# Max-pool and subtract in fp32: a loop by tile, with tiles of five rows in five slots and a first tile in pieces of 1, 1 and 2 rows

## The chip, the cores and the metric

One core of a Trainium2 chip runs the kernel; the other cores are idle. A transfer below is one DMA issue of the kernel. The 16 DMA engines of the core share each transfer, and a packet is what one engine moves at a time: the run of one partition, or the 4-byte completion at the end (in the profile before, 68 transfers make 9792 packets, 9 on each engine per transfer). The metric is the time of one execution on the device in microseconds (us). All times compared here are of undisturbed ("fast") runs unless a sentence says otherwise. The span of a profile, from the first to the last instruction of the program, is some 1.8 us shorter than the time of the same run.

## The reference

```python
x: float32, shape (8, 64, 256, 256)          # B, C, H, W
x_r = x.reshape(B, C, H // 8, 8, W // 8, 8)
pooled = x_r.max(axis=(3, 5))                # maximum of each 8 x 8 window
return x - (pooled repeated 8 times along H and W)
```

Each element is read once (134.2 MB) and written once (134.2 MB). The arithmetic is two passes over data that is on chip.

## The kernel before

Eight image lines form one row of 2048 numbers (8 KB), which holds whole windows. There are 16384 such rows. A tile of *n* rows puts *n* consecutive rows into each of the 128 partitions, so a "row" below means 128 x 8 KB = 1.05 MB. The whole tensor is 128 of these rows: a first tile of four, 30 of four, a last of four.

```python
HEAD = [2, 2]          # pieces of the first tile
SIZE = 4               # rows in a tile
ROUNDS = 5
TAIL = [2, 1, 1]       # pieces of the last tile
SLOTS = 6              # ring: 6 x 4 = 24 rows
...
ring = data.tile([P, SLOTS * SIZE * ROW], F32, name="ring")
```

SyncE issues the loads. It waits for a slot's store before it loads that slot again:

```python
for i in range(len(sizes)):
    slot = slot_of(i)
    if landed[slot]:
        nc.sync.wait_ge(stored[slot], 16 * landed[slot])
    for k, (lo, R) in enumerate(cuts(HEAD if i == 0 else [sizes[i]])):
        ...
        nc.sync.dma_start(out=sbuf(i, lo, R), in_=dram(x_rows, i)[:, part]).then_inc(
            first[k] if i == 0 else loaded[slot], 16)
```

VectorE (DVE) reduces a tile, then subtracts in place, row by row. ScalarE issues a store for each finished tile. TensorE does no matmul; it only passes semaphores on, so that the loop on DVE can wait on one semaphore.

```python
def pool_and_subtract(part, top, R):
    nc.vector.tensor_reduce(out=maxs, in_=wins..., op=max).then_inc(reduced, 1)
    take(reduced, 1)
    for r in range(R):
        sub = nc.vector.tensor_tensor(out=wins[:, r], in0=wins[:, r], in1=maxs[:, r]..., op=subtract)
    sub.then_inc(ready, 1)
...
with nc.vector.Fori(0, ROUNDS):
    with nc.vector.Fori(0, SLOTS) as slot:
        take(filled, 1)
        pool_and_subtract(ring[:, bass.ds(slot * (SIZE * ROW), SIZE * ROW)], ..., SIZE)
```

## Time and profile before

| | before |
|---|---|
| time, median (lowest to highest), first three runs | 627.96 us (627.55 to 628.2) |
| span of the profile | 625.5 us |
| DVE busy | 562.6 us, 90% |
| 16 DMA engines busy (loads 49.9%, stores 49.7%) | 99.6% |
| bytes moved, mean rate | 268.44 MB, 429 GB/s |

What to look at: a resource that is busy 99.6% of the span leaves 0.4% of empty time. Besides filling that, a change can only help it by shortening the work itself. The prediction below shows the lines. One view that it does not show will matter later, the last microseconds in steps of one (columns: stretch, length, DVE busy, POOL busy, clock, DMA share, GB/s):

```profile
622.00:623.00 1.00, 0.00 (x0) 0.00 (x0) 1.00 0.98 418
623.00:624.00 1.00, 0.00 (x0) 0.00 (x0) 1.00 0.28 115
```

All 16 engines work through 622 to 623 and stop within the next microsecond.

### The profile page before, as it was taken

Reading aid. Unit: us, or ns where it says so; the run is one execution under the profiler, and the core shown is the slowest. Engines: PE = TensorE matmul, PEld = TensorE weight load, DVE = VectorE, ACT = ScalarE, POOL = GpSimd, SP = SyncE. Lnnn points to the kernel's source line nnn. Section 1 sums busy time; section 2 is a strip of 40 time slices with the busy share of each in tenths; the row PEclk is TensorE's granted clock in tenths of the full one; section 3 lists DMA queues with packets and bytes.
Section 4 is the critical chain, followed back from the end, with each engine's and each line's share of the span. In section 5 each row is a group of like instructions: output and inputs, shape, how many; then the busy total and the mean of one; then the engine's idle time right before and its main releaser. Section 6 shows DMA issues by size and latency. Waiting matters only on the chain. (4 is left out here: it accounts for less than half of the span.)

```text
span 625.5 us, 613 instructions
## 1 busy us (share of the span) xinstructions
DVE 562.6 (90%) x163; POOL 0.2 (0%) x4
## 2 busy tenths in 40 slices
DVE  4999999998898888988889888898888998888983
POOL 0000000000000000000000000000000000000000
DMA  8999999999999999999999999999999999999998
GB/s 369 402 434 438 436 434 436 434 436 434 434 432 427 425 434 436 436 436 434 436 434 436 434 434 427 430 425 436 436 436 434 436 436 434 434 436 434 425 427 363
DMA packets 9792, 268.44 MB, mean 429 GB/s; under 512 B 1088, under 2 KB 1088, under 8 KB 1088
## 3 DMA queue, kind: packets, MB, share of 16 engines
q1 hardware_dynamic: 4752, 134.22, 49.9%
q10 hardware_dynamic: 5040, 134.22, 49.7%
HBM read 134.22 MB, written 134.22 MB: 429 GB/s over the span
## 5 line engine op out<-in xcount | busy, mean ns | idle before, releaser
L81 DVE TENSOR_REDUCE tops<-ring (+2 forms) x35 | 278.4, 7953 | 48.4 <-DVEq L75 48.4
L93 DVE TENSOR_TENSOR ring<-ring,tops (+1 forms) x128 | 285.0, 2287 | 5.2 <-DVEq L75 0.2
L164 POOL MEMSET const-bfloat16-1.0<- 128x1 bf16 x1 | 0.1, 102 | 0.0
L164 POOL MEMSET const-uint8-127<- 128x1 uint8 x1 | 0.1, 102 | 0.0
L164 POOL MEMSET const-float32-0.0<- 128x1 f32 x1 | 0.1, 99 | 0.2 <-issue 0.2
L164 POOL MEMSET const-float32-1.0<- 128x1 f32 x1 | 0.1, 99 | 0.0
## 6 DMA issues: line engine op xcount, KB each, us to landing
ring<-in_x_dram SPq DMA_DIRECT2D x31, 4096.0 KB, 62.1
out_dram<-ring ACTq DMA_DIRECT2D x30, 4096.0 KB, 35.9
out_dram<-ring ACTq DMA_DIRECT2D x3, 2048.0 KB, 19.3
ring<-in_x_dram SPq DMA_DIRECT2D x2, 2048.0 KB, 9.5
out_dram<-ring ACTq DMA_DIRECT2D x2, 1024.0 KB, 9.2
```

The costliest lines, as they stand in the source:

```text
L81: nc.vector.tensor_reduce(out=maxs if R > 1 else maxs[:, 0], in_=(wins.rearrange("p r ph ow pw -> p r ow ph pw") if R > 1 else wins[:, 0]. ...
L93: sub = nc.vector.tensor_tensor(out=wins[:, r], in0=wins[:, r], in1=maxs[:, r].unsqueeze(1).unsqueeze(3).to_broadcast([P, pH, oW, pW]), op ...
L164: nc = _bacc.Bacc("TRN2", target_bir_lowering=False, num_devices=1)
```

## The change

The intent: start DVE and the first store sooner with smaller first pieces, and use fewer and larger transfers (24 tiles of five rows in place of 30 of four). Five slots of five rows make a ring of 25 rows in place of 24. The nested loop becomes one loop over tiles that works out the slot as a remainder, and the first and last tile are waited for directly in place of the relay through TensorE.

```diff
-HEAD = [2, 2]
-SIZE = 4
-ROUNDS = 5
+HEAD, HEAD_OUT = [1, 1, 2], [2, 2]
+SIZE, TILES = 5, 24
 TAIL = [2, 1, 1]
-SLOTS = 6
+SLOTS = 5
...
-        ).then_inc(reduced, 1)
-        take(reduced, 1)
+        ).then_inc(reduced if nth is None else pooled, 1)
+        if nth is None:
+            take(reduced, 1)
+        else:
+            nc.vector.wait_ge(pooled, nth)
...
-            for lo, R in cuts(HEAD if i == 0 else TAIL if i == last else [SIZE]):
+            for lo, R in cuts(HEAD_OUT if i == 0 else TAIL if i == last else [SIZE]):
...
-        for lo, R in cuts(HEAD):
+        for k, (lo, R) in enumerate(cuts(HEAD)):
+            nc.vector.wait_ge(first[k], 16)
+            pool_and_subtract(sbuf(0, lo, R), top(0, lo, R), R, k + 1)
+        with nc.vector.Fori(0, TILES) as i:
+            slot = i % SLOTS
             take(filled, 1)
...
-        with nc.vector.Fori(0, ROUNDS):
-            with nc.vector.Fori(0, SLOTS) as slot:
```

More of the change, by code (lines that the diff above doesn't have):

```diff
@@ L33 @@
     out_rows = out.rearrange("b c (oh ph) w -> (b c oh) (ph w)", ph=pH)
-    sizes = [sum(HEAD)] + [SIZE] * (ROUNDS * SLOTS) + [sum(TAIL)]
+    sizes = [sum(HEAD)] + [SIZE] * TILES + [sum(TAIL)]
     assert sum(sizes) * P == x_rows.shape[0] and max(sizes) == SIZE
@@ L47 @@
     reduced = tc.alloc_semaphore("reduced")
+    pooled = tc.alloc_semaphore("pooled")
     ready = tc.alloc_semaphore("ready")
@@ L75, in take, with pool_and_subtract @@
         nc.vector.wait_ge(sem, n).then_inc(sem, -n)
-    def pool_and_subtract(part, top, R):
+    def pool_and_subtract(part, top, R, nth=None):
         wins = part.rearrange("p (r ph ow pw) -> p r ph ow pw", r=R, ph=pH, ow=oW)
@@ L112 @@
                 )
-                landed[slot] += 1
-        for k in range(len(HEAD)):
-            nc.tensor.wait_ge(first[k], 16).then_inc(filled, 1)
-        for i in range(1, len(sizes)):
+            landed[slot] += len(HEAD_OUT) if i == 0 else 1
+        for i in range(1, last):
             turn = (i - 1) // SLOTS + 1
@@ L124 @@
         for i in range(len(sizes)):
-            for lo, R in cuts(HEAD if i == 0 else TAIL if i == last else [SIZE]):
+            for lo, R in cuts(HEAD_OUT if i == 0 else TAIL if i == last else [SIZE]):
                 part = slice(lo * ROW, (lo + R) * ROW)
-                done += 1
+                done = [sum(HEAD[: k + 1]) for k in range(len(HEAD))].index(lo + R) + 1 if i == 0 else done + 1
                 nc.scalar.wait_ge(ready, done)
@@ L133 @@
         nc.scalar.wait_ge(final, 16 * n_final)
-        for lo, R in cuts(HEAD):
-            take(filled, 1)
-            pool_and_subtract(sbuf(0, lo, R), top(0, lo, R), R)
-        with nc.vector.Fori(0, ROUNDS):
-            with nc.vector.Fori(0, SLOTS) as slot:
-                take(filled, 1)
-                pool_and_subtract(
-                    ring[:, bass.ds(slot * (SIZE * ROW), SIZE * ROW)],
-                    tops[:, bass.ds(slot * (SIZE * oW), SIZE * oW)],
-                    SIZE,
-                )
-        take(filled, 1)
-        for lo, R in cuts(TAIL):
-            pool_and_subtract(sbuf(last, lo, R), top(last, lo, R), R)
+        for k, (lo, R) in enumerate(cuts(HEAD)):
[3 more added lines that the diff above has]
+            slot = i % SLOTS
+            take(filled, 1)
+            pool_and_subtract(
+                ring[:, bass.ds(slot * (SIZE * ROW), SIZE * ROW)],
+                tops[:, bass.ds(slot * (SIZE * oW), SIZE * oW)],
+                SIZE,
+            )
+        nc.vector.wait_ge(loaded[slot_of(last)], 16 * ((last - 1) // SLOTS + 1))
+        for k, (lo, R) in enumerate(cuts(TAIL)):
+            pool_and_subtract(sbuf(last, lo, R), top(last, lo, R), R, len(HEAD) + k + 1)
 _INS = ['x']
```

## The prediction

> **What bounds the kernel now.** I read the page first, for the busiest resource.
>
> ```profile
> span 625.5 us, 613 instructions
> DVE 562.6 (90%) x163; POOL 0.2 (0%) x4
> ...
> DMA  8999999999999999999999999999999999999998
> GB/s 369 402 434 438 436 434 436 434 436 434 434 432 427 425 434 436 436 436 434 436 434 436 434 434 427 430 425 436 436 436 434 436 436 434 434 436 434 425 427 363
> DMA packets 9792, 268.44 MB, mean 429 GB/s; under 512 B 1088, under 2 KB 1088, under 8 KB 1088
> ...
> q1 hardware_dynamic: 4752, 134.22, 49.9%
> q10 hardware_dynamic: 5040, 134.22, 49.7%
> ...
> ring<-in_x_dram SPq DMA_DIRECT2D x31, 4096.0 KB, 62.1
> out_dram<-ring ACTq DMA_DIRECT2D x30, 4096.0 KB, 35.9
> ```
>
> The load queue (q1) and the store queue (q10) together fill 99.6% of the 16 DMA engines' time, while DVE has 10% to spare. The rate is flat at 434 to 436 GB/s outside the first two slices and the last. Every byte is read once and written once, 268.44 MB, and the change moves the same bytes.
>
> Next, the timeline in steady state, to see whether DVE or the transfers set the pace of a tile.
>
> ```profile
> 142.16 8.90 DVE L93 TENSOR_TENSOR ring<-ring,tops  x4
> 152.70 8.69 DVE L81 TENSOR_REDUCE tops<-ring  x1 [1.64 <-DVEq L75]
> 161.53 8.90 DVE L93 TENSOR_TENSOR ring<-ring,tops  x4
> 172.05 8.69 DVE L81 TENSOR_REDUCE tops<-ring  x1 [1.62 <-DVEq L75]
> ```
>
> From reduce to reduce is 19.35 us. DVE works 161.53 + 8.90 - 152.70 = 17.73 us of it and then waits 1.62 us for the next load. A tile in and out is 8.389 MB; in 19.35 us that is 433.5 GB/s. So the transfers set the pace.
>
> Then the ends of the run, in windows (columns: stretch, length, DVE busy, POOL busy, clock, DMA share, GB/s).
>
> ```profile
> 0.00:2.00 2.00, 0.00 (x0) 0.20 (x4) 1.00 0.11 25
> 2.00:4.00 2.00, 0.00 (x0) 0.00 (x0) 1.00 0.98 311
> ...
> 22.00:24.00 2.00, 1.99 (x1) 0.00 (x0) 1.00 0.60 246
> ```
>
> ```profile
> 620.00:622.00 2.00, 0.00 (x0) 0.00 (x0) 1.00 1.04 438
> 622.00:624.00 2.00, 0.00 (x0) 0.00 (x0) 1.00 0.63 266
> 624.00:626.00 2.00, 0.00 (x0) 0.00 (x0) 1.00 0.00 0
> ```
>
> The DMA engines start by 2 us, dip once when stores join near 22 us, and stop near 624 us. DVE ends at 616.2 us, earlier than the transfers, so the listed chain of waits (its last piece is a DVE subtraction at 613.92) is not what ends the run: the drain of stores is.
>
> **What the Trainium skill says.** "DMA: Bandwidth & Descriptors", Where 436 GB/s comes from, gives a fabric ceiling of 435.2 GB/s; it also says that for HBM transfers a lower limit of about 358 binds. The trace agrees with the ceiling (436 in most slices) and not with the lower limit. The same page, Why small descriptors are slow, names a fixed cost of about 3 cycles per packet; I size that from this trace below. Its section Queues, rings and completion order says that each DMA engine takes turns between its queues packet by packet. The trace agrees: while 2-row stores (16 KB packets) stand against 4-row loads (32 KB packets), the first store is issued at 17.57 us and lands 19.3 us later, at 36.9; the second, issued at 26.53, lands 24.9 us later, at 51.4. The 14.5 us between them are six row times of 2.41 us (1.049 MB at 435.2 GB/s): two rows out beside four in, not two beside two. "VectorE: DVE Perf Modes" gives 2291 ns for an fp32 two-tensor operation on 2048 elements; the trace has 2287.
>
> **The change part by part.**
>
> Bytes: at 435.2 GB/s they need 268.44/0.4352 = 616.8 us. The 8.7 us above that in the span are some 1.9 at the start, 1.5 at the end (last packet to end of span), and about 5 of packet costs and disturbance. Nothing in the change touches the 616.8.
>
> Packets: each DMA gives each of 16 engines eight data packets (one per partition) and one 4-byte packet for the semaphore. Before: 33 loads and 35 stores, 68 x 9 = 612 packets per engine, and 612 x 16 = 9792, the page's number. After: 28 loads (1, 1, 2 rows, 24 of five, one of four) and 29 stores (2, 2, 24 of five, 2, 1, 1), 57 x 9 = 513. The cost of one, an estimate: a steady tile takes 19.35 us against 8.389/0.4352 = 19.28, so 0.07 to 0.09 us for its 18 packets, 4 to 5 ns each. The packet records of the trace give an upper figure: medians 309, 611 and 1213 ns for 8, 16 and 32 KB leave 9 ns at zero size. 99 packets fewer save 0.5 to 0.9 us. This lies directly on the bounding resource. I take 0.7.
>
> DVE, steady: reduces of 1, 2 and 4 rows took 2278, 4417 and 8685 ns, 2.13 us a row and 0.15 fixed; a further subtraction adds 2.20 (8.90 less 2.287, over 3). Five rows: 17.73 + 2.13 + 2.20 = 22.07 us, against a transfer period of 10.486/0.4352 + 0.08 = 24.17. DVE keeps 2.1 us of slack per tile, so the register remainder for the slot costs nothing unless it exceeds that. Reduces fall from 35 to 30, saving 5 x 0.15 = 0.7 us of DVE, off the path.
>
> Head: the first load carries one row instead of two and lands 2.41 us sooner. DVE starts at 8.47 - 2.41 = 6.06, takes two one-row pieces at 4.63 (the spacing of such pieces in the tail), and the first store goes out near 6.06 + 9.26 + 0.1 = 15.4 instead of 17.57. This is the part meant to gain; but until then loads already keep the DMA engines at 0.98 or more. An earlier store only swaps which bytes move first. Worth 0. Replacing the relay of the semaphore through PE by a direct wait is off the path as well.
>
> Ring: 25 rows instead of 24. One row is on average resident for (rows in ring) x 4.84 us: before 116.2, and 62.1 + 17.7 + 35.9 = 115.7 accounts for it. After: 121, of which 22.1 on DVE, so 98.9 remain for the two queues. Each transfer needs only 24.2 at half rate, 48.4 for both; some 50 us are spare and neither queue runs dry. The division between queues is made in the head: stores start 0.9 row earlier, but 16 KB packets now stand against 40 KB ones, so the four head rows leave beside ten rows in, not eight. About one row more waits to be stored; nothing in time.
>
> Tail: same pieces. The last one-row store took 9.2 us to land; alone it would need about 2.41 plus 2.7 of latency (the first load: 7.5 us for 4.8 us of transfer), 5.1. So 4 us of DVE lateness are hidden. The last load of four rows passes beside five rows of stores, (4+5) x 2.41 = 21.7 us, a little under DVE's 22.07: 0.4 us of lateness, hidden.
>
> Sum: -0.7 + 0 + 0 + 0 = -0.7 us; 627.96 - 0.7 = 627.3.
>
> **The rivals.**
>
> The head gain is real: the run ends 2.2 us sooner, 625.8 with no other part. For it: slices 1 and 2 show only 369 and 402 GB/s. Against: those losses are the start before the first packet and the dip when stores join; neither is waiting for DVE.
>
> The 40 KB run is cut in two, or is slower per byte. Then 24 x 2 x 8 = 384 more packets per engine at 4 to 9 ns, 1.5 to 3.5 us, net +1 to +3: about 629.3. For: no run of 40 KB was seen yet. Against: 8, 16 and 32 KB scale in a line.
>
> The coarser ring starves loads: with five tiles, a late store delays 5 MB. If each of some 20 tiles lost 1 us, 647. For: the loads already wait for stores in most of the run. Against: 62.1 us from issue to landing is 3.2 tiles queued.
>
> DVE or the tail binds: if the loop's added register work took over 2.1 us per tile, each further us would cost 24 us in all; if the backlog at the end were two rows smaller, the tail would be bound by DVE, +1 to 2 us. Against: the slack computed above.
>
> **Range and chances.** Three runs of before lie within 0.65 us, so the noise is half as large as the effect. The packet estimate and the head gain pull down to 626; the two mild rivals up to 629. Range 626.0 to 628.8. A gain over 2% would need 615.4 us, under the 616.8 of the bytes alone: 1%. A loss over 2% needs 640.5, which only starvation or a DVE bound gives: 2%.
>
> **What the profile after would show.** Packets 57 x 144 = 8208 and under 512 B 912; if the run is cut, 8208 + 6144. DVE 158 instructions and about 561.9 us busy; first reduce near 6.1 us, first store near 15.4; landings of the first two stores about seven row times, 16.9 us, apart if turns are by packet. Reduce to reduce 24.2 us with about 2.1 idle. Loads some 60 us from issue to landing and stores 37 to 40. Middle slices still 434 to 436 GB/s; last packets near 623. I am wrong on mechanism if the middle rate changes, if the DMA share falls below 0.98 in the middle, or if DVE's end and the end of the span come closer than about 5.5 us.

## The result, and the profile after

| | before | changed |
|---|---|---|
| time, median of 6 runs (lowest to highest) | 627.48 us (627.32 to 628.2) | 628.88 us (627.23 to 629.33) |
| span of the profile | 625.5 us | 627.1 us |

The ratio of the changed kernel to the kernel before is 1.0017, with a 95% interval of 1.0005 to 1.003. (A ratio is the mean time of one kernel's fast runs over that of the other's of the same rounds, so it is not quite the ratio of the medians.) By the 2% rule the two are the same. That is the class the prediction held for likely (97%). In microseconds it is at the upper edge of the predicted range of 626.0 to 628.8: the ratio puts it at 1.0017 x 627.48 = 628.5, the median of 628.88 is a hair above. The sign is not the predicted one: -0.7 us was expected and about +1 came. Five of the six runs lie between 628.78 and 629.33, one at 627.23: a spread of 2.1 us, where the six runs of before spread over 0.9.

The page of the changed kernel:

```profile
span 627.1 us, 559 instructions
DVE 561.3 (90%) x158; POOL 0.2 (0%) x4
...
GB/s 390 392 423 453 423 426 452 418 444 431 421 455 421 423 455 418 444 434 418 455 421 421 457 421 436 439 421 452 423 421 457 421 436 439 421 449 433 428 421 312
DMA packets 8208, 268.44 MB, mean 428 GB/s; under 512 B 912, under 2 KB 912, under 8 KB 912
...
q1 hardware_dynamic: 4032, 134.22, 49.8%
q10 hardware_dynamic: 4176, 134.22, 49.5%
...
ring<-in_x_dram SPq DMA_DIRECT2D x24, 5120.0 KB, 60.5
out_dram<-ring ACTq DMA_DIRECT2D x24, 5120.0 KB, 37.9
```

There are 8208 packets and 912 small ones, as counted ahead of the run, so a run of 40 KB stays one packet. DVE is as busy as forecast (561.3 against 561.9). The rate by slice now swings between 418 and 457. That comes of counting whole packets: with the bytes of each packet spread over its duration, every slice from the third to the last but one has 433 or 434 GB/s, before and after. The last slice fell from 363 to 312. Steady state and head, from the timeline:

```profile
163.82 10.82 DVE L81 TENSOR_REDUCE tops<-ring  x1 [2.11 <-DVEq L75]
...
188.05 10.82 DVE L81 TENSOR_REDUCE tops<-ring  x1 [2.15 <-DVEq L75]
```

```profile
5.89 2.29 DVE L81 TENSOR_REDUCE tops<-ring 128x32 f32<-128x2048 f32 x1 [5.89 <-DMA ring<-in_x_dram]
...
15.06 37.09 ACTq L130 DMA_DIRECT2D out_dram<-ring  x3
...
29.71 10.82 DVE L81 TENSOR_REDUCE tops<-ring  x1 [5.83 <-DVEq L75]
```

From reduce to reduce is 24.23 us with 2.15 us of waiting. DVE begins at 5.89 us and the first store is issued at 15.06 us. DVE then loses most of its lead: it waits 5.83 us for the first five-row tile, which lands as a whole only at 29.2 us. Now the end:

```profile
622.00:623.00 1.00, 0.00 (x0) 0.00 (x0) 1.00 0.82 344
623.00:624.00 1.00, 0.00 (x0) 0.00 (x0) 1.00 0.08 33
624.00:625.00 1.00, 0.00 (x0) 0.00 (x0) 1.00 0.06 25
625.00:626.00 1.00, 0.00 (x0) 0.00 (x0) 1.00 0.02 8
```

This is the reading that the rest rests on. In 622 to 623 less is left to do than before (0.82 against 0.98): most engines end sooner, as forecast. But then a share of 0.06 goes on for almost two microseconds, and 0.06 is 1/16: one DMA engine of the 16 is working alone. A transfer counts as landed when its slowest engine is done, so the run waits for it.

The packet records of the trace (start and length of every packet) give the same in numbers. Fifteen engines end between 622.81 and 623.26 us and the sixteenth at 625.47. Before, all sixteen end between 623.19 and 624.01. In every profile that is read here, the last engine's end plus 1.4 to 1.6 us is the span.

The lag is not made at the end. Each transfer posts 16 completions, one per engine; the time from the first to the sixteenth shows how far the engines are out of step. The largest such spread in each stretch of 50 us:

```
stretch (us)              60-110  150-200  250-300  350-400  450-500  550-600
before, us                  2.0     2.0      2.0      2.0      2.0      2.0
changed, us                 2.0     2.5      3.6      4.1      4.2      4.3
```

In the changed kernel the fifteen other completions are up to 1.4 us apart until 200 us, and from then on stay within about 0.6 us of each other. In its records nine load packets after 60 us, and no store packet, are more than 20 ns longer than the 1514 ns that nearly all 40 KB packets take; the excess is 0.06 to 0.47 us each and 2.15 us in all. The records do not name the engine of a packet, but an engine starts its next packet within a few ns of the end of the one before. Followed back in this way from the last packet, the chain has the right bytes but for one packet too many at its very start, and all nine slow packets are on it: they belong to the engine that ends late. In the kernel before no load packet after 60 us is late by 20 ns. In the first 60 us, while the ring fills, both kernels have many such packets (57 of before, late by 22.6 us in all, and 79 of the changed kernel, by 21.7 us), so slow load packets as such are not peculiar to the change.

### The profile page after: what moved, and what is told of

Same layout as the page of the kernel before. It is cut to its first block, busy times and chain, and to the rows that moved or that the text cites. A ratio compares the mean times of both kernels' runs of the same rounds, so it can differ in the third digit from the quotient of the medians.

```text
span 627.1 us, 559 instructions
## 1 busy us (share of the span) xinstructions
DVE 561.3 (90%) x158; POOL 0.2 (0%) x4
## 2 busy tenths in 40 slices
DMA packets 8208, 268.44 MB, mean 428 GB/s; under 512 B 912, under 2 KB 912, under 8 KB 912
## 6 DMA issues: line engine op xcount, KB each, us to landing
ring<-in_x_dram SPq DMA_DIRECT2D x24, 5120.0 KB, 60.5
out_dram<-ring ACTq DMA_DIRECT2D x24, 5120.0 KB, 37.9
```

## The experiments

Theory A: the packet saving is real on every engine, and one engine falls behind by about 2 us in most executions of the changed kernel; the end waits for it. Theory B: the change carries a fixed cost, in the new head or in the larger transfers, the same in every run. Runs of one call share a chip and the runs of the kernel before: the first call is the first repeat, the head alone, the first run of five-row tiles and the price of a packet; the second is the third set, the second run of five-row tiles, and six and eight rows; the third is the rest.

### The changed kernel again

No edit.

> The changed kernel again, unedited, to see whether its two levels (one run of 627.2 among five of 628.8 to 629.3) come back. Theory A (one of the 16 DMA engines falls some 2 us behind the others in most executions; the rest end about 0.7 us earlier than before): most runs 628.5 to 629.5, a few near 627.2, and the profile ends with a window in which the DMA share is about 0.06, one engine of 16. Theory B (the new head or the larger transfers cost a fixed time): all runs at one level near 628.9, all engines ending late together.

Measured: 627.15 us (626.77 to 627.45) against 627.19 of before; ratio 0.9997 (0.9984 to 1.0011). Last microseconds:

```profile
622.00:623.00 1.00, 0.00 (x0) 0.00 (x0) 1.00 0.70 295
623.00:624.00 1.00, 0.00 (x0) 0.00 (x0) 1.00 0.06 25
```

The late engine is gone, or nearly: the last ends at 623.76, the median one at 622.78. The same program thus gave 628.9 in one set of runs and 627.15 in another, which speaks against a fixed cost. Neither theory had foreseen that all five runs would be at the lower level.

### The changed kernel a third time

No edit; another chip.

> The changed kernel a third time, unedited. Its first runs held one DMA engine that ended 2.2 us after the other fifteen; the repeat did not (it ended 0.2 us after the next). If the straggler belongs to chance at the start of an execution or to a chip: this run is at one of the two levels, 627.2 or about 629, and the profile's last windows show one engine of 16 alone at the upper level and not at the lower. If the first result was an ordinary fixed cost of the change: 628.9.

Measured: 627.78 us (627.22 to 628.89); ratio 1.0011 (0.9998 to 1.0024). The five runs fall into 627.22 to 627.78 and 628.62 to 628.89, so the levels alternate on one chip and are not merely two chips. The profiled run is between them (span 626.0):

```profile
623.00:624.00 1.00, 0.00 (x0) 0.00 (x0) 1.00 0.06 25
624.00:625.00 1.00, 0.00 (x0) 0.00 (x0) 1.00 0.02 8
```

One engine ends at 624.39 and the next at 623.26: a lag of 1.1 us, between the 0.2 and 2.2 us of the other two profiles. Three profiles, three lags, and each span is the last engine's end plus 1.5 to 1.6.

### The head alone

```diff
-SIZE, TILES = 5, 24
+SIZE, TILES = 4, 30
-SLOTS = 5
+SLOTS = 6
```

(edits here are against the changed kernel, unless said otherwise)

> The loop by tile and the head in pieces of 1, 1 and 2 rows alone: tiles of four rows in six slots as before. Packets 69 x 9 = 621 per engine, 9 more than before. If the head costs (theory B): about 628.5 to 629. If the head is worth 0 and the straggler comes with the five-row tiles (theory A): 627.3 to 628.0, within 0.1% of before, and no single engine that ends later than the rest by over 1 us. If the early first store were a gain: 625.5.

Measured: 627.39 us (627.01 to 627.52) against 627.19; ratio 0.9999 (0.9985 to 1.0012). The loop by tile, the direct waits and the early first store are together worth nothing, neither gain nor loss. All engines end between 623.39 and 624.13, and no load packet after 60 us is late by 20 ns. But in this call the whole changed kernel had no late engine either (the first repeat above), so the run does not tell whether the head alone can bring one.

### Five-row tiles alone

```diff
-HEAD, HEAD_OUT = [1, 1, 2], [2, 2]
+HEAD, HEAD_OUT = [2, 2], [2, 2]
```

> Five-row tiles in five slots with the old head of two pieces of two rows: 56 x 9 = 504 packets per engine. Theory A: the straggler comes with five-row tiles whatever the head, so 627.0 to 629.3, in two levels or the upper one. Theory B: without the small pieces the packet saving shows, 626.6 to 627.2 in all runs.

Measured: 626.69 us (626.59 to 626.79) against 627.19; ratio 0.999 (0.9977 to 1.0004). Repeated on another chip:

> Five-row tiles with the old head, repeated. Packet theory: 108 packets per engine fewer than before at 5.0 ns (the split run: 2.75 us for 549 more) is -0.54 us, so 626.7 or 0.999 of before, all runs within 0.3 us. If the straggler belongs to five-row tiles whatever the head: some runs 1 to 2 us higher.

Measured: 626.62 us (626.6 to 626.72) against 627.25; ratio 0.9988 (0.9975 to 1.0001). The end of the first of the two:

```profile
622.00:623.00 1.00, 0.00 (x0) 0.00 (x0) 1.00 0.68 287
623.00:624.00 1.00, 0.00 (x0) 0.00 (x0) 1.00 0.02 8
```

Ten runs lie within 0.2 us of each other, all below the lowest run of before in the same call (626.95 and 626.98). This is the fastest version found, by 0.5 to 0.6 us, though each interval still just takes in 1. The completions of a transfer stay within 0.8 us of each other all the way. These are the times that theory B forecast; theory A had expected the late engine here. What speaks against B are the repeats of the changed kernel, not this run. So five-row tiles with the old head ran ten times without a late engine. That it takes five-row tiles and the small first pieces together is suggested by this and not shown: in the first call the changed kernel had no late engine either, and in the second it was at the upper level in two runs of five, against none of five here.

### The price of a packet

The kernel before, with every load, and every store but the last tile's, cut in two.

```diff
-            for k, (lo, R) in enumerate(cuts(HEAD if i == 0 else [sizes[i]])):
+            for k, (lo, R) in enumerate(cuts(HEAD if i == 0 else [2, 2])):
...
-            nc.tensor.wait_ge(loaded[slot_of(i)], 16 * turn).then_inc(filled, 1)
+            nc.tensor.wait_ge(loaded[slot_of(i)], 32 * turn).then_inc(filled, 1)
```

(and the same cut for the stores)

> The kernel before with every four-row load and store (except the tail's stores) split into two DMAs of two rows: 64 loads and 65 stores, 129 x 9 = 1161 packets per engine against 612, each of 16 KB. It measures the cost of a packet. At 4 to 9 ns a packet as predicted: +2.2 to +4.9 us, 629.7 to 632.4. If packets cost nothing: 627.5, and then the predicted saving of 0.7 us never existed.

Measured: 629.94 us (629.84 to 630.53) against 627.19; ratio 1.0044 (1.003 to 1.0058).

```profile
DMA packets 18576, 268.44 MB, mean 427 GB/s; under 512 B 2064, under 2 KB 2064, under 8 KB 2064
```

18576/16 = 1161 packets per engine, 549 more, cost 629.94 - 627.19 = 2.75 us: 5.0 ns each (3.4 to 6.6 over the interval of the ratio), an average over eight data packets and one completion per transfer. The changed kernel has 99 fewer, so 0.50 us is what it can save by this, and five-row tiles alone (108 fewer) should save 0.54. They saved 0.50 and 0.63. A caution: the run with six rows and stores cut, below, has as many packets as before and still came out 0.40 lower, so half a microsecond is near what such a comparison can tell.

### Six rows in four slots

Old head of two pieces, 24 rows of ring. (From here to the runs with one direction cut, the versions have `HEAD, HEAD_OUT = [2, 2], [2, 2]`; that line and the counts of semaphores are cut from the diffs.)

```diff
-SIZE, TILES = 5, 24
+SIZE, TILES = 6, 20
-SLOTS = 5
+SLOTS = 4
```

> Tiles of six rows in four slots (24 rows of ring), old head: 23 loads and 25 stores, 48 x 9 = 432 packets per engine, 180 fewer than before. Packet theory: -0.90 us, about 626.3. Starved ring: DVE needs 26.4 us of a 29.0 us period, and the ring holds 24 x 4.84 = 116 us against 58 for two transfers and 26 for DVE, 32 us spare: no starvation, so a time over 628 would speak for it.

Measured: 629.98 us (629.29 to 631.36) against 627.25; ratio 1.0045 (1.0032 to 1.0058). A miss: the saving of 0.9 us became a loss of 2.7.

```profile
624.00:626.00 2.00, 0.00 (x0) 0.00 (x0) 1.00 0.14 57
626.00:628.00 2.00, 0.00 (x0) 0.00 (x0) 1.00 0.02 8
```

A share of 0.14 is two engines and a little: three of them end at 624.33, 626.18 and 626.78, the others by 623.73. Late engines are back in greater number, and with the old head. 35 load packets after 60 us are late, by 9.7 us in all (a later expectation says 12.7). The completions of a transfer are up to 6.3 us apart.

### Eight rows in three slots

```diff
-SIZE, TILES = 5, 24
+SIZE, TILES = 8, 15
-SLOTS = 5
+SLOTS = 3
```

> Tiles of eight rows in three slots, old head: 18 loads and 20 stores, 38 x 9 = 342 packets per engine, 270 fewer, if a run of 64 KB stays one packet: -1.35 us, 625.8, when only packets count. Ring theory: the ring holds 116.2 us, two transfers at half rate need 77.1 and DVE 35.2, together 112.3, so only 3.9 us are left[...]: this ring is at its limit, and any further wait shows as DMA share under 0.98 in the middle and a time of 628 to 650.

Measured: three fast runs of 651.71, 651.97 and 652.47 us against 627.25; ratio 1.039 (1.0372 to 1.0408). Four more runs of 668.75 to 675.33 count as slow (over 1.5% above the fastest). Their granted clock was 1.0 like that of the others, so they may as well be a scatter of this kernel's own. The ring's limit that the expectation computed shows, and 64 KB packets may add to it, so the two were separated: the same tiles with transfers of four rows.

```diff
+LOADS, STORES = [4, 4], [4, 4]
 SLOTS = 3
...
-            for k, (lo, R) in enumerate(cuts(HEAD if i == 0 else [sizes[i]])):
+            for k, (lo, R) in enumerate(cuts(HEAD if i == 0 else [sizes[i]] if i == last else LOADS)):
```

> Eight-row tiles in three slots, as the run that lost 4%, but each load and store goes as two DMAs of four rows, packets of 32 KB: 612 per engine, as before. If the coarse ring (three slots, 3.9 us spare) costs the time: 650 or more stays. If packets of 64 KB are what is slow: near 627.3 and DMA packets at their normal length. A part of both: 630 to 645.

Measured: 650.91 us (650.43 to 653.89) against 627.62; ratio 1.0376 (1.0363 to 1.039). Packets of 32 KB, 612 per engine as in the kernel before, and the loss stays: it does not need long packets, which leaves the ring of three large tiles. The ring's waits are not all of it, though. Per engine, the packets of this run took 9.3 us more beyond the usual length of their size than those of before (271 load packets after 60 us are late, by 139.8 us in all), and the engines idled some 17 us more; together that is the 26.6 us by which its span is longer. Why the packets are slow here is as open as in the changed kernel. What DVE waited for, and a window near the end:

```profile
DVE tops L82 <- DVEq L76: 68.3, 12, 13.8
```

```profile
610.00:620.00 10.00, 10.00 (x5) 0.00 (x0) 1.00 0.00 0
```

From 610 to 620 us DVE works without a pause on the last eight-row tile while no engine moves a byte: every store that was ready has gone. This is what a bound by DVE at the tail looks like; it has no counterpart in the changed kernel.

### Six rows, with one direction cut in two

Both versions have 612 packets per engine, the number of the kernel before. Only loads in two pieces:

```diff
-SIZE, TILES = 5, 24
+SIZE, TILES = 6, 20
+LOADS, STORES = [3, 3], [SIZE]
-SLOTS = 5
+SLOTS = 4
```

> Six-row tiles in four slots with only the loads in two DMAs of three rows (24 KB packets), stores whole (48 KB). The unsplit kernel took 629.98 with some 12.7 us of slow load packets in all on a few engines. If the length of the load packet is what makes it slow: 627.0 to 627.6 (612 packets, as before) and few slow packets. If the length of the store packet that a load stands beside is: still 629 to 631.

Only stores in two pieces:

```diff
+LOADS, STORES = [SIZE], [3, 3]
```

> The other half: six-row tiles, loads whole (48 KB packets), only the stores in two DMAs of three rows (24 KB). If the load packet's own length makes it slow: 629 to 631 with slow load packets as before. If the store packet's length beside it does: 627.0 to 627.6. Taking turns by packet, loads of 48 KB beside stores of 24 KB get two thirds of the time, so the ring fills until loads wait for slots; that in itself should not change the sum.

Measured with loads cut: 663.03 us (660.21 to 672.92, of which the highest counts as slow; 661.92 is the median of the five others) against 627.62; ratio 1.0566 (1.0541 to 1.059). With stores cut: 627.22 us (626.86 to 627.46); ratio 0.9993 (0.9981 to 1.0006). Transfers of the first (columns: issue, number, KB, us from issue to landing), then what its DVE waited for, then two stretches near its end:

```profile
ring<-in_x_dram SPq DMA_DIRECT2D x40, 3072.0 KB, 54.8
out_dram<-ring ACTq DMA_DIRECT2D x20, 6144.0 KB, 27.6
```

```profile
DVE tops L82 <- DVEq L76: 77.6, 15, 14.9
```

```profile
600.00:620.00 20.00, 16.18 (x3) 0.00 (x0) 1.00 0.81 346
620.00:640.00 20.00, 19.97 (x9) 0.00 (x0) 1.00 0.49 209
```

The same of the second:

```profile
ring<-in_x_dram SPq DMA_DIRECT2D x20, 6144.0 KB, 25.9
out_dram<-ring ACTq DMA_DIRECT2D x40, 3072.0 KB, 49.0
```

```profile
DVE tops L82 <- DVEq L76: 31.6, 11, 5.1
```

The following is a reading of these numbers, not shown step by step. If a DMA engine takes turns by packet, as the first two stores do (17 us apart, see below), the direction with the longer packets gets more of the time. With long stores (48 KB beside 24 KB) the ring is full of loads that have not landed (54.8 us), stores go out as fast as they come (27.6 us, less than the 29 us that a six-row store needs at half the rate), and nothing is in reserve: a load that one engine delivers late stops DVE at once (77.6 us of waiting). There the completions of one transfer were up to 38.6 us apart. With long loads, rows land early (25.9 us) and wait to be stored (49.0 us); DVE does not care that a load's completions are up to 3.0 us apart. The packet records show where the 32.9 us went by which the profiled span with loads cut is longer. Until 600 us the engines hardly idle; their packets are slow, loads and stores (273 and 307 late ones after 60 us), which makes 14.9 us per engine beyond before. After 600 us one engine is still bringing the last loads, until 631.1, and from 618 us on the others are nearly all out of work: 14.7 us of idle time more than before, per engine. The rest, 3.3 us, is idle time earlier. Why the packets are slow stays open, and so it is not shown that the missing reserve makes all of the loss. Neither expectation had this: the run with loads cut was thought to cure or keep a loss of 2.7 us, and it cost 34.3 (fast runs alone). That the longer load packet in itself makes the loss of the six-row kernel is refuted by the run with stores cut, which has 48 KB loads and no loss, though 24 load packets in it are late by 3.1 us in all.

### The first store later

The small first loads are kept, but the first tile is stored once, whole.

```diff
-HEAD, HEAD_OUT = [1, 1, 2], [2, 2]
+HEAD, HEAD_OUT = [1, 1, 2], [4]
```

> The changed kernel with the same first loads of 1, 1 and 2 rows, but the first tile stored once, whole, at about 24 us instead of two stores from 15 us: 504 packets per engine. If the first small loads are what throws one engine out of step: two levels, 627 to 629, and an engine that ends over 1 us late in the profile. If it is where the first small store meets the five-row loads: 626.5 to 626.9 in all runs.

Measured: 629.56 us (627.12 to 630.62) against 627.62; ratio 1.002 (1.0003 to 1.0037). Two levels again: 627.12 and 627.28 in two runs, 629.05 to 630.62 in four.

```profile
600.00:605.00 5.00, 5.00 (x3) 0.00 (x0) 1.00 0.40 172
```

Here all engines but one end together (626.54 to 626.72, the last at 627.37), and the time is lost earlier: between 600 and 605 us they are busy only 0.40 of the time. Once more one engine has fallen behind (load completions 1.0 us apart near 70 us, 4.4 from 290 us on, and the fifteen others within 0.9). The last five-row load is complete at 581.1, 4.4 us after its first engine is done. DVE, which waits for it, passes the delay on to its next store, at 603.6, and the other engines have run out of stores by 601.5 to 602.3. So the time of the first two-row store is not what makes the late engine, and the small first loads are not cleared. This run also changed the size of the first store, so it does not convict them.

## Why the prediction was right or wrong

**Bytes bound the time: right.** DMA engines stayed at 99.3% in the changed kernel, and from 60 to 560 us the rate was 434 GB/s (433 before). Two readings under it were loose. The trace has 436 in 14 of 40 slices, not in most, and with packets spread over their duration the steady rate is 433, just under the ceiling of 435.2. And the dip near 22 us was no idle time: the engines were full, but 32 load packets between 18 and 25 us were late, by 12.7 us in all. Of the versions run, all but those that left no reserve (three slots, or stores with the longer packets) lie within 0.5% of before.

**Packets: right in size, smaller than the number taken.** The count was exact, and the price of 5.0 ns is inside the 4 to 9 ns of the estimate. The term should have been -0.50, not -0.7: the steady tile had given 4 to 5 ns, so 0.4 to 0.5, and the upper figure of the packet records pulled it up. It shows on the fifteen engines, whose median end moved from 623.38 to 622.97, and in both runs of five-row tiles with the old head.

**DVE: right.** Period 24.23 us (24.17 forecast), idle 2.15 (2.1), total 561.3 (561.9). The remainder for the slot cost nothing that can be seen.

**Head worth nothing: right by itself.** DVE began at 5.89 and the store went out at 15.06 (6.06 and 15.4 forecast), and the head alone gave 0.9999. That turns go by packet was confirmed closely by the first two stores. From the transfers issued before 20 us, and then from those issued between 20 and 60 us:

```profile
out_dram<-ring ACTq DMA_DIRECT2D x1, 2048.0 KB, 22.0
```

```profile
out_dram<-ring ACTq DMA_DIRECT2D x1, 2048.0 KB, 30.1
```

Issued at 15.06 and 23.91 us, they land at 37.1 and 54.0: 17 us apart, where seven row times (16.9 us) were forecast.

**Ring and tail: right.** Loads took 60.5 us and stores 37.9 (some 60, and 37 to 40). DVE ended at 616.6 and the span at 627.1, so the tail was not bound by DVE.

**The sum failed in a term that it did not have.** "Sum: -0.7 + 0 + 0 + 0" treats 16 engines as one. The signs that the prediction named as proof of its error did not come (the printed slices left its 434 to 436, but the rate did not change, see above; the DMA share stayed at 1.00; DVE ended 10.5 us before the span); what came was one of its milder forecasts failing, "last packets near 623", which held for fifteen engines and was 2.4 us off for the sixteenth. The step to add is the lag of the slowest engine: 2.2 us beyond the next one in the profiled run, 0.2 and 1.1 in two others. In numbers: the median engine ends 0.41 us sooner than before (622.97 for 623.38), and the last one follows it after 2.50 us in place of 0.63, 1.87 more. Together +1.46 us; the medians of the times differ by 1.4 (628.88 - 627.48). That the time still fell at the edge of the range is luck. The upper end was opened for two rivals that did not come: no run was cut (8208 packets), and DVE did not bind the tail. The late engine, which was in no term, happened to cost about as much. (The cut rival's own sum, +1 to +3, would even lie above the range.) The rival "slower per byte" is thus true for nine packets on one engine and false for the 40 KB packet as such: nearly all took 1514 ns, five times 301 ns plus 9, as the shorter ones had led one to expect.

**What stays open.** Why one engine's load packets are slow, why only in some executions, and why the lag stops growing near 300 us. The late engine came with five-row tiles behind a first tile loaded in pieces of 1, 1 and 2 (at different strength in three profiles of the changed kernel, 7 of whose 16 runs are at the upper level, and in the run with a late store). It was not seen with either part alone, but the head alone ran only where the changed kernel was free of it too, so this is no proof that it takes both. With six-row tiles it came, on three engines, behind the old head as well. In the versions with four or more slots and both directions whole, it was seen at 40 and 48 KB and not at 32; that packet length is the cause is not shown by this, since the tile and the ring change with it, and the eight-row run with 32 KB packets had 271 slow load packets and completions up to 5.7 us apart. Nor is the fault found for the small first loads: no run took them away one by one.

## What to carry to other kernels

Where the DMA engines are full from the first load on, an earlier start of compute or of the first store was worth nothing, and a packet saved about 5 ns; five-row tiles with the old head took some 0.5 us off, near the limit of what these runs can tell, and no version did better. Look at the engines singly, not at their mean: a DMA share of 0.06 that lasts is one engine of 16, and the slowest engine sets both the landing of a transfer and the end of the run. Before choosing the sizes of loads and stores, work out which direction has the longer packets (0.9993 with longer loads, 1.0566 with longer stores, the number of packets being the same); that the reserve of landed rows, which hides a late engine, makes the difference is the likely reading; and leave room in the ring beyond load, compute and store (three slots of eight rows: 1.0376).

## What the Trainium skill lacked or had wrong

- "DMA: Bandwidth & Descriptors", Where 436 GB/s comes from: it says that for transfers between HBM and SBUF the HBM side, about 358 GB/s, binds. With one core at work the runs show 433 and 434 GB/s (before and changed, 60 to 560 us) for loads and stores mixed.
- The same page, Why small descriptors are slow: it gives a cost per packet in cycles and calls it a matter of small descriptors. In these runs a packet costs 5.0 ns at 16 to 32 KB as well (549 more per engine: 2.75 us).
- The same page, Queues, rings and completion order: it says that engines take turns by packet, but not what follows from unequal packets. With six-row tiles, cutting only the loads in two cost 5.7%, cutting only the stores nothing (ratios 1.0566 and 0.9993).
- No page has it: with packets of 40 to 48 KB in both directions one to three of the 16 engines fell behind by 1 to 3.5 us in some runs, by single slow load packets, each late by up to 0.47 us in the changed kernel. ("DMA: Bandwidth & Descriptors", Latency and other measured facts, calls two of the engines usually slower in traces, without a number; these records do not name the engine of a packet, so they cannot be compared with that.)
